# Tile starts at multiples of 256 bytes, and products that stream their columns backwards

## The chip, the cores and the metric

The kernel runs on one core of a Trainium2 chip. The metric is the device time of one execution in microseconds (us); lower is better. Five engines work beside each other, each with its own queue of instructions, and wait for one another through semaphores: TensorE (PE; its weight loads are listed as PEld), VectorE (DVE), ScalarE (ACT), GpSimd (POOL) and SyncE (SP), which issues the DMA transfers. SBUF is the on-chip memory of 128 partitions in which tiles lie; PSUM is the memory into which TensorE writes its products.

## The reference

Two layers of a hybrid block over a sequence of 512 positions and 1024 features, in float32. In each layer x gets, one after the other, the (normed) output of a mixer and of a feed-forward:

```python
for l in range(DEPTH):                       # DEPTH = 2
    mixed = hybrid_mixer(rms_norm(x, mix_pre_g[l]), w_in[l], ..., w_out[l])
    x = x + rms_norm(mixed, mix_post_g[l])
    ff = conv_ffn(rms_norm(x, ffn_pre_g[l]), w_up[l], conv_w[l], conv_b[l], w_down[l])
    x = x + rms_norm(ff, ffn_post_g[l])
```

`hybrid_mixer` projects to 3600 columns (`w_in`), runs dilated attention with 8 heads over one half and a bidirectional mLSTM with 4 heads over the other, and projects back with `w_out` (1024 x 1024). `conv_ffn` projects to 5632 columns (`w_up`), convolves three neighbouring positions, takes gelu(gate) * value and projects the 2816 columns back (`w_down`).

## The kernel before

Activations lie transposed: features on the 128 partitions, the 512 positions along the free dimension. The matrix x is 8 such tiles, `w_up` makes 44 of them, and so on. A weight tile of 128 x 1024 (8 blocks of 128 x 128) comes by DMA into a ring of three (`wraw`); ScalarE rounds it to a high part (`whi`, line 153) and VectorE subtracts that to get a low part (`wlo`, line 91), both float32r. Activations are split in the same way: `ah`/`al` (made in `parts_of`) for the two projections that read x, `cp` for the output projection, `hh`/`hl` for the 22 hidden tiles of the feed-forward. A product of full precision is then three matmuls, in `mac` (lines 200 to 202): weights high x moving high, weights low x moving high, weights high x moving low, all accumulating in one PSUM tile (`mm`, `o`, `s` or `t`, each one bank of 512 float32 columns). Each of the three loads its own 128 x 128 weights first.

`mac` runs with 512 columns in most places, and with `cols`, a half of 256 columns, in `first_group` (the first tiles after a norm) and `last_tiles` (the last tiles ahead of a norm), so that norm work of one half lies beside products of the other. The value projection (`proj_v`, lines 896 to 898) is the other way round: there the activations are the stationary operand and two weight blocks side by side (256 columns) are the moving one. The remaining matmuls are written out where they are used: gates (454, 456), attention scores (713, 714), transposes (730 and others), attention output (756), the mLSTM (787 to 839), the sums of squares (314) and the row of norm factors (329).

The order of the work is written by hand. `mac` calls `settle()`, which issues the norm steps that have come due by a count of streamed columns; two `Stream` objects feed pieces of attention and mLSTM work between the projections' matmuls in the mixer (`pump`). The feed-forward is a plain loop over tiles, in which VectorE and ScalarE do the convolution and the gelu of one pair of tiles under the products of the next.

Tiles come from pools. A pool takes its tiles in the order in which they are first asked for, each right behind the last, with starts at multiples of 32 bytes. The pools that matter here are `const`, `base` (x, `ah`, `al`), `wraw_p`, `whi_p`, `wlo_p`, `sm`, and one pool for each mixer (`mp`) and each feed-forward (`fp`, with `hh` and `hl`). The first tiles in `const` are two of 276 float32 per partition (`prm`, 1104 bytes), so most later tiles do not start at a multiple of 256 bytes.

Of the kernel before, what the change touches and what calls it, by code (L numbers as in the profile page):

```python
# [8 lines left out]
F32 = mybir.dt.float32  # L9
# [7 lines left out]
P = 128  # L17
# [6 lines left out]
FT = FF // P  # L24
EPS = 1e-6
RAW = 3
RING = 3
HD = 128
KSC = HD ** -0.5
# [25 lines left out]
NC1 = CC["rowmask"]  # L55


@with_exitstack
def tile_hybrid_block(ctx: ExitStack, tc: tile.TileContext, xt, w_in, w_g, w_out, w_up, w_down, par, cst, out):
    nc = tc.nc  # L60
    pool = lambda name, bufs=1, **kw: ctx.enter_context(tc.tile_pool(name=name, bufs=bufs, **kw))
    const = pool("const")
    base = pool("base")
    wraw_p = pool("wraw", RAW)
    whi_p = pool("whi", RING)
    wlo_p = pool("wlo", RING)
    sm = pool("sm", 2)
    pp = pool("pp", space=PSUM)

    def mm_ps():  # L70
        return pp.tile([P, T], F32, tag="mm", bufs=3, name="mm")
# [7 lines left out]
    def s_ps():  # L79
        return pp.tile([P, T], F32, tag="s", bufs=2, name="s")  # L80
# [4 lines left out]
    def o_ps():  # L85
        return pp.tile([P, T], F32, tag="o", bufs=1, name="o")
# [85 lines left out]
    def take():  # L172
        return ready.popleft() if ready else split_w()

    def prefetch(n):
        while len(ready) < n and raw_q:
            ready.append(split_w())
# [8 lines left out]
    def settle(all=False):  # L186
        due.sort(key=lambda e: e[0])
        while due and (all or due[0][0] <= clock[0]):
            with tc.issue_after(clock[1]):
                due.pop(0)[1]()  # L190

    def mac(ps, w, kk, rhs, first, last, cols=None):

        settle()
        clock[0] += 3 * (T if cols is None else cols.stop - cols.start)
        hi, lo = w[kk]
        rh, rl = rhs
        if cols is not None:
            rh, rl = rh[:, cols], rl[:, cols]
        nc.tensor.matmul(out=ps, lhsT=hi, rhs=rh, start=first, stop=False)  # L200
        nc.tensor.matmul(out=ps, lhsT=lo, rhs=rh, start=False, stop=False)  # L201
        clock[1] = nc.tensor.matmul(out=ps, lhsT=hi, rhs=rl, start=False, stop=last).ins  # L202


    class Stream:


        def __init__(self, rate):
            self.normal = rate
            self.gens = deque()  # L210
            self.due = 0.0
# [202 lines left out]
    def first_group(ws, pss, xp, scale, extra=None):  # L414

        for hf in range(2):
            cols = halves[hf]
            for k in range(KT):
                if hf == 1 and k == 0:
                    scale.go(0)  # L420
                if extra is not None:
                    extra(k, cols)
                for w, ps in zip(ws, pss):
                    mac(ps[:, cols], w, k, xp[k], k == 0, k == KT - 1, cols)
# [21 lines left out]
    def mixer_first(l, xp, sp, G, more, whole=False):  # L446
        gps = mm_ps()
        wg = wgs[l]
        ws = [take() for _ in range(G)]
        pss = [mm_ps() if m < 2 else o_ps() for m in range(G)]  # L450
        scale = PreScale(sp() if callable(sp) else sp)

        def gate_macs(k, cols):
            nc.tensor.matmul(out=gps[0:32, cols], lhsT=wg[:, k, 0:32], rhs=xp[k][0][:, cols], start=(k == 0), stop=False,
                             skip_group_check=True)
            nc.tensor.matmul(out=gps[0:16, cols], lhsT=wg[:, k, 0:16], rhs=xp[k][1][:, cols], start=False,
                             stop=(k == KT - 1), skip_group_check=True)

        if whole:

            for k in range(KT):
                if k == 5:
                    scale.go(0)
                    scale.go(1)
                gate_macs(k, slice(0, T))
                for w, ps in zip(ws, pss):
                    mac(ps, w, k, xp[k], k == 0, k == KT - 1)
        else:
            first_group(ws, pss, xp, scale, gate_macs)
        if more:  # L470
            scale.go(1)
            w = take()
            prefetch(RING - 1)
            ps = s_ps()
            for k in range(KT):
                mac(ps, w, k, xp[k], k == 0, k == KT - 1)
            pss.append(ps)
            settle(True)
        return gps, pss, scale, more or whole

    def mixer(l, xp, first, mp, post):
# [21 lines left out]
        def scale_ready():  # L503
            settle(True)
            if not more:
                scale.sums(1)
                scale.rows(1)
            nc.vector.tensor_tensor(out=cosr, in0=cosr, in1=scale.row, op=ALU.mult)
            nc.vector.tensor_tensor(out=sinr, in0=sinr, in1=scale.row, op=ALU.mult)
# [352 lines left out]

        prefetch(RING - 1)
        scale_ready()
# [5 lines left out]
        def proj():  # L870
            if pss:
                return pss.pop(0)
            w = take()
            prefetch(RING - 1)
            ps = mm_ps()
            for k in range(KT):
                mac(ps, w, k, xp[k], k == 0, k == KT - 1)
                M.pump()
                A.pump()
            return ps  # L880

        def proj_v():

            ws = [take()["all"] for _ in range(2)]
            prefetch(1)
            vps = []
            for c in range(4):
                if c % 2 == 0:
                    vps.append(mm_ps())
                o_ = vps[-1][:, (c % 2) * 2 * P:(c % 2 + 1) * 2 * P]  # L890
                for k in range(KT):
                    hi, lo = (w[:, 2 * (k % 4):2 * (k % 4) + 2, :].rearrange("p i f -> p (i f)") for w in ws[k // 4])
                    xh, xl = (t[:, c * P:(c + 1) * P] for t in xp[k])
                    settle()
                    clock[0] += 6 * P
                    nc.tensor.matmul(out=o_, lhsT=xh, rhs=hi, start=(k == 0), stop=False)  # L896
                    nc.tensor.matmul(out=o_, lhsT=xh, rhs=lo, start=False, stop=False)  # L897
                    clock[1] = nc.tensor.matmul(out=o_, lhsT=xl, rhs=hi, start=False, stop=(k == KT - 1)).ins  # L898
                    if k % 2:
                        M.pump()  # L900
                        A.pump()
            return vps

        M.start(gates(gps), .6)
        for r in range(4):
            done = set()
            for c in ORDER[r]:
                if c == "V":
                    vps = proj_v()
                    M.run()  # L910
                    A.run()
                    v_out(vps)
                elif c in "qk":
                    conv_out(proj(), r + 4 * (c == "k"), "m" + c)
                else:
                    ps = proj()
                    A.run()
                    rot_out(ps, "aq" if c == "a" else "ak")
                done.add(c)
                if done >= set("qkV") and "M" not in done:  # L920
                    M.run()
                    M.start(mlstm(r))
                    done.add("M")
                if done >= set("abV") and "A" not in done:
                    A.start(attn(r), AR[r])
                    done.add("A")
        for r in range(4):
            ps = proj()
# [49 lines left out]
        for m in range(G):  # L978
            mac(pss[m], ws[m], order[7], cp[order[7]], False, True)
        prefetch(RING)  # L980
        for m in range(G):
# [6 lines left out]
        for m in range(G, KT - 2):  # L988
            w = take()
            ps = o_ps() if m == G else mm_ps()  # L990
# [26 lines left out]
    def ffn_first(post):  # L1017
        ws = [take() for _ in range(FG)]
        pss = [mm4_ps() for _ in range(FG)]
        scale = PreScale(post.st2)  # L1020
        xp = post.ops
        first_group(ws, pss, xp, scale)
        return pss, scale
# [114 lines left out]
        gains(l)  # L1138
    first = None
    for l in range(DEPTH):  # L1140
        with tc.tile_pool(name=f"mix{l}", bufs=1) as mp:
            post = Post(l, "mix_post", l, "ffn_pre", 2)
            if first is None:
                first = mixer_first(l, xp, sp, 2, False, True)
            mixer(l, xp, first, mp, post)
            first = ffn_first(post)
            xp = post.ops
        with tc.tile_pool(name=f"ffn{l}", bufs=1) as fp:
            post = Post(l, "ffn_post", l + 1, "mix_pre", 1)
            ffn(l, xp, first, fp, post)  # L1150
            xp, sp = post.ops, lambda p=post: p.st2
            if l + 1 < DEPTH:
                first = mixer_first(l + 1, xp, sp, 2, False)
# [99 lines left out]
```

## Time and profile before

| | |
|---|---|
| time, median of 2 runs | 1366.78 us (1366.04 to 1367.51) |
| profiled execution, its own time | 1366.06 us |
| its span, first to last instruction | 1364.3 us |
| granted TensorE clock, mean | 0.998 |
| PE busy | 1329.2 us, 97% of the span, 7152 matmuls |
| PEld busy (weight loads, beside the matmuls) | 1127.2 us, 83% |
| VectorE busy | 955.4 us, 70% |
| ScalarE busy | 719.4 us, 53% |
| DMA | 115.34 MB, mean 85 GB/s |

The profile comes from one execution. In its timeline a row gives the start and the duration in us, the engine, the line of the kernel, the operation, the tile written and the tiles read, and the shape. Matmuls are pipelined and their ends are modelled, so the records of consecutive matmuls overlap; the distance between two starts says how long one occupies TensorE. The list of groups gives for each line and form the number of instructions, their busy time and the mean duration.

### The profile page before, as it was taken

What the parts mean: (1) busy time and instruction counts of PE and PEld (TensorE: products, weight loads), DVE (VectorE), ACT (ScalarE), POOL (GpSimd) and SP (SyncE); (2) the same over time, 40 slices, a digit from 0 to 9 for tenths busy, and PEclk for the clock granted to TensorE, in tenths of its full rate; (3) what the DMA queues carried; (4) which work ended last, traced back from release to release, by engine and by line L of the source; (5) the groups of instructions that cost most, each with busy time, mean ns of one, the idle gap of its engine ahead of it and who ended that gap; (6) DMA issues with size and microseconds to landing.
All of it is one profiled execution on the core that took longest, in us unless ns stands there. A gap on an engine that the chain in (4) does not pass through costs nothing. (4 is left out here: it accounts for less than half of the span.)

```text
span 1364.3 us, 18689 instructions
## 1 busy us (share of the span) xinstructions
PE 1329.2 (97%) x7152; PEld 1127.2 (83%) x7152; DVE 955.4 (70%) x1885; ACT 719.4 (53%) x1226; POOL 109.4 (8%) x116
## 2 busy tenths in 40 slices
PE   7999999999999999999989999999999999999997
PEld 6788879889888888888977888888898888888886
DVE  6999888847887777422499998887469777763233
ACT  5596696654644444323346867966446444442220
POOL 0000100024000000001130001000330000000002
PEclk9999999999999999999999999999999999999999
DMA  6212112241233333333222222122313333332321
GB/s 235 63 47 78 35 58 78 73 128 46 68 103 104 97 93 91 98 87 110 94 69 62 62 63 62 47 79 82 104 47 94 106 95 93 96 101 86 97 85 62
DMA packets 34089, 115.34 MB, mean 85 GB/s; under 512 B 3664, under 2 KB 6352, under 8 KB 34000
## 3 DMA queue, kind: packets, MB, share of 16 engines
q1 hardware_dynamic: 34000, 114.15, 27.6%
q8 instruction: 56, 0.92, 0.3%
q14 instruction: 33, 0.27, 0.1%
HBM read 112.04 MB, written 2.10 MB: 84 GB/s over the span
## 5 line engine op out<-in xcount | busy, mean ns | idle before, releaser
L91 DVE TENSOR_TENSOR wlo<-wraw,whi 128x1024 fp32r<-128x1024 f32 (+1 forms) x192 | 236.6, 1235 | 179.5 <-ACT whi L153 177.6
L200 PE MATMUL mm<-ah,whi 128*128 128x512 f32 (+1 forms) x880 | 336.4, 383 | 0.0
L201 PE MATMUL mm<-ah,wlo 128*128 128x512 f32 (+1 forms) x880 | 334.1, 380 | 0.0
L202 PE MATMUL mm<-al,whi 128*128 128x512 f32 (+1 forms) x880 | 332.9, 379 | 0.9 <-DVE al L348 0.8
L153 ACT CAST whi<-wraw 128x1024 fp32r<-128x1024 f32 (+1 forms) x192 | 197.6, 1034 | 166.7 <-PE mm L202 111.0
L202 PEld LDWEIGHTS mm<-al,whi 128*128 128x128 f32 x880 | 165.8, 189 | 30.5 <-DVE al L348 1.7
L200 PEld LDWEIGHTS mm<-ah,whi 128*128 128x128 f32 x880 | 166.2, 189 | 29.2 <-ACT whi L153 0.5
L201 PEld LDWEIGHTS mm<-ah,wlo 128*128 128x128 f32 x880 | 166.1, 189 | 27.5
L296 POOL TENSOR_TENSOR acc<-acc,sq 128x512 f32<-128x512 f32 x22 | 29.6, 1345 | 758.8 <-ACT sq L293 754.6
L201 PE MATMUL mm<-hh,wlo 128*128 128x512 f32 x220 | 86.8, 395 | 0.0
L202 PE MATMUL mm<-hl,whi 128*128 128x512 f32 x220 | 86.8, 395 | 0.0
L200 PE MATMUL mm<-hh,whi 128*128 128x512 f32 x220 | 86.8, 395 | 0.0
L1032 DVE TENSOR_TENSOR u<-mm,prow 128x512 f32<-128x512 f32 x64 | 43.8, 687 | 50.1 <-PE mm L202 39.6
L896 PE MATMUL mm<-whi,ah 128*128 128x256 f32 x256 | 73.6, 289 | 0.2 <-DVE cu L634 0.2
L1049 ACT CAST hh<-cv 128x512 fp32r<-128x512 f32 x44 | 27.3, 621 | 87.5 <-DVE cv L1046 87.5
L898 PE MATMUL mm<-whi,al 128*128 128x256 f32 x256 | 72.5, 284 | 0.0
L897 PE MATMUL mm<-wlo,ah 128*128 128x256 f32 x256 | 72.5, 283 | 0.0
L1044 ACT ACTIVATE cg<-cg 128x512 f32<-128x512 f32 x44 | 27.9, 633 | 74.5 <-DVE cg L1038 74.3
L201 PE MATMUL o<-ah,wlo 128*128 128x512 f32 (+1 forms) x160 | 60.7, 379 | 0.0
L202 PE MATMUL o<-al,whi 128*128 128x512 f32 (+1 forms) x160 | 60.6, 379 | 0.0
L200 PE MATMUL o<-ah,whi 128*128 128x512 f32 (+1 forms) x160 | 60.6, 379 | 0.0
L722 ACT ACTIVATE p<-p,mx 128x512 f32<-128x512 f32 x64 | 46.1, 720 | 18.0 <-DVE mx L719 17.9
(320 smaller groups left out, 2786.5 us busy)
## 6 DMA issues: line engine op xcount, KB each, us to landing
wraw<-in_w_up SPq DMA_DIRECT2D x88, 512.0 KB, 3.6
wraw<-in_w_in SPq DMA_DIRECT2D x56, 512.0 KB, 3.6
wraw<-in_w_down SPq DMA_DIRECT2D x32, 512.0 KB, 3.5
wraw<-in_w_out SPq DMA_DIRECT2D x16, 512.0 KB, 3.6
wraw<-in_w_down SPq DMA_DIRECT2D x16, 384.0 KB, 3.1
x<-in_xt SPq DMA_DIRECT2D x4, 512.0 KB, 7.0
out_dram<-x SPq DMA_DIRECT2D x8, 256.0 KB, 2.2
tb<-in_cst SPq DMA_DIRECT2D x2, 967.0 KB, 5.1
```

The lines of the kernel that those rows point to most:

```text
L91: nc.vector.tensor_tensor(out=dst, in0=src, in1=f32v(hi), op=ALU.subtract)
L153: nc.scalar.copy(out=hi[:, 0:m, :], in_=raw[:, k:k + m, :])
L200: nc.tensor.matmul(out=ps, lhsT=hi, rhs=rh, start=first, stop=False)
L201: nc.tensor.matmul(out=ps, lhsT=lo, rhs=rh, start=False, stop=False)
L202: clock[1] = nc.tensor.matmul(out=ps, lhsT=hi, rhs=rl, start=False, stop=last).ins
L296: e.tensor_tensor(out=self.acc[:, cols], in0=self.acc[:, cols], in1=sq, op=ALU.add)
L722: nc.scalar.activation(out=p_, in_=p_, func=AF.Exp, scale=-1.0, bias=mx, accum_out=den)
L896: nc.tensor.matmul(out=o_, lhsT=xh, rhs=hi, start=(k == 0), stop=False)
L897: nc.tensor.matmul(out=o_, lhsT=xh, rhs=lo, start=False, stop=False)
L898: clock[1] = nc.tensor.matmul(out=o_, lhsT=xl, rhs=hi, start=False, stop=(k == KT - 1)).ins
L1032: nc.vector.tensor_tensor(out=u, in0=ps, in1=st["row"], op=ALU.mult)
L1044: nc.scalar.activation(out=g, in_=g, func=AF.Gelu_apprx_tanh)
```

## The change

Three things change. A small class `Lines` stands between the code and the pools: it sends tiles of less than 256 bytes per partition to a pool of their own, rounds the size of the others up to a multiple of 256 bytes, and so makes each of them begin at a multiple of 256 (three filler tiles move the pools' beginnings to such a multiple). The matmuls of `mac` get their output, and both their moving operands, as reversed views (`[:, ::-1]`): the last column is read first and written first, and every column still goes to its own place. The matmuls of `proj_v` get the same. The stationary operands and all other matmuls stay as they are.

```diff
--- before.py
+++ after.py
@@ -24,6 +24,7 @@
 FT = FF // P
 EPS = 1e-6
 RAW = 3
+LINE = 256
 RING = 3
 HD = 128
 KSC = HD ** -0.5
@@ -55,16 +56,39 @@
 NC1 = CC["rowmask"]
 
 
+class Lines:
+
+
+    def __init__(self, pool, small, bufs=1):
+        self.pool, self.small, self.bufs = pool, small, bufs
+
+    def tile(self, shape, dtype, bufs=None, **kw):
+        bufs = bufs or self.bufs
+        n = 1
+        for s in shape[1:]:
+            n *= s
+        if n * 4 < LINE:
+            return self.small.tile(shape, dtype, bufs=bufs, **kw)
+        if n * 4 % LINE == 0:
+            return self.pool.tile(shape, dtype, bufs=bufs, **kw)
+        flat = self.pool.tile([shape[0], -(-n * 4 // LINE) * LINE // 4], dtype, bufs=bufs, **kw)[:, 0:n]
+        if len(shape) == 2:
+            return flat
+        names = "abcd"[:len(shape) - 1]
+        return flat.rearrange(f"p ({' '.join(names)}) -> p {' '.join(names)}", **dict(zip(names, shape[1:-1])))
+
+
 @with_exitstack
 def tile_hybrid_block(ctx: ExitStack, tc: tile.TileContext, xt, w_in, w_g, w_out, w_up, w_down, par, cst, out):
     nc = tc.nc
-    pool = lambda name, bufs=1, **kw: ctx.enter_context(tc.tile_pool(name=name, bufs=bufs, **kw))
-    const = pool("const")
-    base = pool("base")
-    wraw_p = pool("wraw", RAW)
-    whi_p = pool("whi", RING)
-    wlo_p = pool("wlo", RING)
-    sm = pool("sm", 2)
+    pool = lambda name, **kw: ctx.enter_context(tc.tile_pool(name=name, bufs=1, **kw))
+    big, small = pool("big"), pool("small")
+
+    big.tile([P, 32], F32, name="fill")
+    small.tile([P, 56], F32, name="fill_small")
+    const, sm = Lines(big, small), Lines(big, small, 2)
+    base = const
+    wraw_p, whi_p, wlo_p = Lines(big, small, RAW), Lines(big, small, RING), Lines(big, small, RING)
     pp = pool("pp", space=PSUM)
 
     def mm_ps():
@@ -197,6 +221,8 @@
         rh, rl = rhs
         if cols is not None:
             rh, rl = rh[:, cols], rl[:, cols]
+
+        ps, rh, rl = ps[:, ::-1], rh[:, ::-1], rl[:, ::-1]
         nc.tensor.matmul(out=ps, lhsT=hi, rhs=rh, start=first, stop=False)
         nc.tensor.matmul(out=ps, lhsT=lo, rhs=rh, start=False, stop=False)
         clock[1] = nc.tensor.matmul(out=ps, lhsT=hi, rhs=rl, start=False, stop=last).ins
@@ -887,12 +913,13 @@
             for c in range(4):
                 if c % 2 == 0:
                     vps.append(mm_ps())
-                o_ = vps[-1][:, (c % 2) * 2 * P:(c % 2 + 1) * 2 * P]
                 for k in range(KT):
+                    o_ = vps[-1][:, (c % 2) * 2 * P:(c % 2 + 1) * 2 * P]
                     hi, lo = (w[:, 2 * (k % 4):2 * (k % 4) + 2, :].rearrange("p i f -> p (i f)") for w in ws[k // 4])
                     xh, xl = (t[:, c * P:(c + 1) * P] for t in xp[k])
                     settle()
                     clock[0] += 6 * P
+                    o_, hi, lo = o_[:, ::-1], hi[:, ::-1], lo[:, ::-1]
                     nc.tensor.matmul(out=o_, lhsT=xh, rhs=hi, start=(k == 0), stop=False)
                     nc.tensor.matmul(out=o_, lhsT=xh, rhs=lo, start=False, stop=False)
                     clock[1] = nc.tensor.matmul(out=o_, lhsT=xl, rhs=hi, start=False, stop=(k == KT - 1)).ins
@@ -1138,14 +1165,18 @@
         gains(l)
     first = None
     for l in range(DEPTH):
-        with tc.tile_pool(name=f"mix{l}", bufs=1) as mp:
+        with tc.tile_pool(name=f"mix{l}", bufs=1) as mb, tc.tile_pool(name=f"mixs{l}", bufs=1) as ms:
+            mp = Lines(mb, ms)
             post = Post(l, "mix_post", l, "ffn_pre", 2)
             if first is None:
                 first = mixer_first(l, xp, sp, 2, False, True)
             mixer(l, xp, first, mp, post)
             first = ffn_first(post)
             xp = post.ops
-        with tc.tile_pool(name=f"ffn{l}", bufs=1) as fp:
+        with tc.tile_pool(name=f"ffn{l}", bufs=1) as fb:
+            fp = Lines(fb, fb)
+            if l == 1:
+                fb.tile([P, 16], F32, name="fill_ffn")
             post = Post(l, "ffn_post", l + 1, "mix_pre", 1)
             ffn(l, xp, first, fp, post)
             xp, sp = post.ops, lambda p=post: p.st2
```

## The prediction

> **What bounds the kernel now.** I read the top of the page first, then who TensorE waited for, then the matmuls in order of time.
>
> ```profile
> span 1364.3 us, 18689 instructions
> PE 1329.2 (97%) x7152; PEld 1127.2 (83%) x7152; DVE 955.4 (70%) x1885; ACT 719.4 (53%) x1226; POOL 109.4 (8%) x116
> PEclk9999999999999999999999999999999999999999
> ```
>
> TensorE is busy 97% of the span at a full granted clock; VectorE, next, 70%. The profiled execution took 1366.06 us, its span 1364.3 us, so 1.8 us lie around it; the median of the runs, 1366.78 us, is 0.7 us higher. I count from 1366.06.
>
> ```profile
> PE mm L454 <- ACT ah L347: 8.6, 3, 7.1
> PE s L329 <- DVE rs_y L266: 4.6, 4, 2.0
> PE t L562 <- DVE U L560: 3.3, 2, 1.7
> ```
>
> These are TensorE's largest waits (total us, times, longest): 7.1 us is the start, before the first activations exist, and the rest are norm and gate chains. Nothing there is worth 2%. What remains is the pace of the matmuls. The duration column doesn't give it, since records overlap; the distance between starts does. Here are first and last rows of four unbroken stretches.
>
> ```profile
> 460.14 0.39 PE L200 MATMUL mm<-ah,whi 128*128 128x512 f32 x1
> ...
> 465.35 0.39 PE L202 MATMUL mm<-al,whi 128*128 128x512 f32 x1
> 600.22 0.40 PE L200 MATMUL mm<-hh,whi 128*128 128x512 f32 x1
> ...
> 605.82 0.40 PE L200 MATMUL mm<-hh,whi 128*128 128x512 f32 x1
> 704.44 0.28 PE L896 MATMUL mm<-whi,ah 128*128 128x256 f32 x1
> ...
> 705.99 0.28 PE L897 MATMUL mm<-wlo,ah 128*128 128x256 f32 x1
> 661.33 0.28 PE L202 MATMUL mm<-hl,wlh 128*128 128x256 f32 x1
> ...
> 664.05 0.28 PE L202 MATMUL mm<-hl,wlh 128*128 128x256 f32 x1
> ```
>
> Up projection: 5.21 us over 23 steps, **226.5 ns** per 512-column product. Down projection: 5.60 us over 24 steps, **233.3 ns** for the same shape. Value projection: 1.55 us over 13 steps, **119.2 ns** per 256 columns. Last tile of the down projection: 2.72 us over 24 steps, **113.3 ns**. So one shape has two paces, 6.8 ns apart at 512 columns and 5.9 at 256, at one clock and with no wait. What differs between the first two stretches is where the tiles lie. Adding up the pools' tiles in the code, ah, al, whi and wlo start 160 bytes past a multiple of 256, while hh and hl start 96 past. And it is not the address alone:
>
> ```profile
> 668.62 0.28 PE L201 MATMUL o<-hh,wll 128*128 128x256 f32 x1
> ...
> 669.09 0.28 PE L202 MATMUL o<-hl,wlh 128*128 128x256 f32 x1
> 460.14 0.19 PEld L201 LDWEIGHTS mm<-ah,wlo 128*128 128x128 f32 x1
> ```
>
> The same form over the same kind of tiles now steps 0.47 us in 4, 117.5 ns, after other products had come between. The load of the next weights starts with the product (460.14, as in the matmul row above). Two streams that start together, each reading its own tile, whose joint pace depends on their addresses and can lock at two values: I read this as the weight load holding up the moving read a fixed number of times per product, each worth some 6.7 ns. That is my inference; no row names it.
>
> **The change part by part.** It removes and adds no instruction, DMA or semaphore; no step is moved past a queue and no wait is added. `Lines` only changes where tiles begin, and `[::-1]` only the direction in which `mac` and the value projection stream. The same columns reach the same places, and who reads the output waits for the end of the group as before.
>
> How many products are turned:
>
> ```profile
> 0.00:1364.00 1364.00, 622.00 (x1660) 312.89 (x1660) 1.00 0.28 85
> L200 PE MATMUL mm<-ah,whi 128*128 128x512 f32 x768 | 304.4, 396 | 0.0
> L200 PE MATMUL mm<-hh,whi 128*128 128x512 f32 x220 | 86.8, 395 | 0.0
> L200 PE MATMUL o<-ah,whi 128*128 128x512 f32 x144 | 56.1, 390 | 0.0
> L200 PE MATMUL o<-hh,whi 128*128 128x512 f32 x88 | 34.7, 394 | 0.0
> L200 PE MATMUL mm<-cp,whi 128*128 128x512 f32 x80 | 31.5, 398 | 0.0
> L896 PE MATMUL mm<-whi,ah 128*128 128x256 f32 x256 | 73.6, 289 | 0.2 <-DVE cu L634 0.2
> ```
>
> The first row is L200's alone over the whole span (busy of products and of weight loads, with counts): 1660. The five 512-column rows hold 768 + 220 + 144 + 88 + 80 = 1300; the other 360 I count as 256 columns wide (a few small groups are not, which moves the sum by under 0.5 us). L201 and L202 have as many, so 3900 wide products, 3 x (220 + 88) = 924 of them at 233.3 ns (hh, hl) and 2976 at 226.5, and 3 x 360 + 3 x 256 = 1848 narrow ones. Scores, transposes, gate products and the mLSTM's are not turned.
>
> *Alignment alone.* It gives moving tile and weights the same start modulo 256, as the up projection has today (160 and 160). Least: the 924 of hh and hl drop to 226.5 ns, 924 x 6.8 = 6.3 us. It could also cost: no row has both at 0, and the locking shows that pairs count; the other end is that the other 2976 take 233.3 ns, 2976 x 6.8 = 20 us lost.
>
> *Direction.* No product in the trace reads backwards. The nearest rows are a scan pair on VectorE, one forward, one with all operands reversed:
>
> ```profile
> L569 DVE TENSOR_TENSOR_SCAN cm<-ut x2: 412/413/414, 54.5 to 729.7; 32x128 f32<-32x128 f32 x2
> L570 DVE TENSOR_TENSOR_SCAN cb<-ut x2: 388/388/389, 54.9 to 730.1; 32x128 f32<-32x128 f32 x2
> ```
>
> Reversed is 388 ns against 413: a backward walk over fp32 in SBUF costs nothing by itself there. So I take direction to change only how the moving read meets the weight read. From above it is bounded by two steps: 226.5 - 2 x 6.7 = 213 ns; from below by two steps the other way, 240 ns. Which of them no row decides. I take **one step better than the best pace seen**, 220 ns wide, and for narrow ones the best pace seen, 113.3 ns, because it is the value nearest to the rows among those in which direction does anything good, and because with one start for all tiles every pair meets alike, so that one pace must hold for all. That its sign is a gain is a choice: the rows show that meetings cost, not which direction has fewer.
>
> Sum: 2976 x 6.5 = 19.3 us; 924 x 13.3 = 12.3; narrow, without the 264 of the last down tiles (which already touch 113.3), 1584 x 5.9 = 9.3; those 264 at half of 117.5 - 113.3, 0.6. Together 41.5 us.
>
> *What is late next.*
>
> ```profile
> 40.00:180.00 140.00, 134.90 (x804) 114.94 (x802) 126.69 (x310) 102.60 (x198) 9.49 (x6) 1.00 0.21 61
> 330.00:530.00 200.00, 200.00 (x905) 166.48 (x904) 151.32 (x208) 93.95 (x118) 0.00 (x0) 1.00 0.32 96
> 695.00:870.00 175.00, 167.78 (x1036) 144.27 (x1035) 157.25 (x394) 126.08 (x246) 13.51 (x14) 1.00 0.22 65
> ```
>
> Busy us by stage of PE, PEld, DVE, ACT, POOL. In the mixers (first and third row) VectorE is busy 126.69 of 140 us and 157.25 of 175, about 90%: faster products there run into its chains. About a thousand products are turned in these two stretches, so some 6 us of gain lie there; I let a third be lost, 2 us. In the feed-forward (second row) VectorE has a quarter of the time free, so the gain stays.
>
> Other engines: I expect no change of theirs from the new addresses.
>
> ```profile
> L153 ACT CAST whi<-wraw x192: 832/1051/1079, 8.1 to 1321.3; 128x1024 fp32r<-128x1024 f32 x178, 128x768 fp32r<-128x768 f32 x14
> L153 ACT CAST pth<-wraw x4: 1047/1048/1050, 268.1 to 948.4; 128x1024 fp32r<-128x1024 f32 x4
> wraw<-in_w_up SPq DMA_DIRECT2D x88, 512.0 KB, 3.6
> ```
>
> The same cast takes 1051 ns into whi (160 past) and 1048 into pth (192 past). Weight transfers land in 3.6 us, while a block of 24 products at 226.5 ns takes 5.4: hidden, and still hidden at 5.3. Without that cover a late block would stall TensorE for the difference. At the start the 7.1 us wait may move by some tenths.
>
> Result: 1366.06 - 41.5 + 2 = **1327 us**. Its own range: with 213 ns, 2976 x 13.2 + 924 x 20 + 9.9 - 2 = 65.7 us, 1300; and 1339, 2% below today, where it passes into the next case. (2%, 27 us, is about what a measurement of this kernel tells from no change.)
>
> **The rivals.**
>
> *A: direction does nothing*, alignment levels the paces: 924 x 6.8 = 6.3 us, perhaps 10 more if the narrow ones go to 113.3: 1350 to 1360. For it: the scan rows, and that up projections already have equal offsets and still need 226.5. [...] That the change doesn't do what it says (tiles of one pool off the grid) also ends here, near 1366.
>
> *B, slower: the backward read meets the weight read more often.* Two streams that move towards each other meet more often than two in one direction, if the load runs upwards. Place: every turned product. Two steps, 240 ns: 2976 x 13.5 + 924 x 6.7 + 1848 x 5.9 = 57 us, 1423; one step, 233.3: 20 + 11 = 31 us, 1397. It is slower by 2% once the mean cost passes 27 us / 5748 = 4.8 ns per turned product.
>
> *C, much slower: the output side doesn't take descending columns at full rate.* No row bounds it; at half rate 3900 x 226.5 ns = 883 us more, 2250 us. The scan rows speak against it, but they write SBUF, not an accumulating PSUM bank. [...]
>
> **How the numbers follow.** Forecast 50%; A 24% and the change without effect 2%; B 17%; C 7%. Faster by over 2%: 0.50; within 2%: 0.26; slower: 0.24. The range 1300 to 1400 takes in the forecast, A, and B with one step (8 of its 17), leaving out B's second step, C and some of the forecast's lower tail: about 80%.
>
> **What would show it.** Wide starts in both projections of the feed-forward at one distance: 220 ns right, 226.5 rival A, 233 or 240 B, over 400 C. The narrow ones at 113. VectorE's and ScalarE's durations unchanged, and their waits for TensorE shorter. The prediction is wrong if the up and down projection still differ (addresses aren't what sets the pace), or if the wide pace falls and the span doesn't, which would put the loss into TensorE's waits in the mixers.

## The result and the profile after

The changed kernel takes **1380.70 us** (median of 2 runs, 1379.93 to 1381.46) against 1366.78; the ratio is 1.0104 (95% interval 1.0087 to 1.0121). It is slower by 1%, well outside the noise, where 1327 us, 3% faster, had been forecast. The profiled execution took 1379.93 us, 13.9 us more than the one before.

The head of the page of the changed kernel and TensorE's largest wait (total us, times, longest us):

```profile
span 1377.9 us, 18691 instructions
PE 1344.9 (98%) x7152; PEld 1127.8 (82%) x7152; DVE 955.8 (69%) x1885; ACT 715.6 (52%) x1226; POOL 108.7 (8%) x116
PEclk9999999999999999999999999999999999999999
PE mm L480 <- ACT ah L373: 8.2, 3, 6.7
```

TensorE is busy 15.7 us longer with the same 7152 matmuls, at the same granted clock (0.998); its largest waits are what they were (the first 8.2 us against 8.6, the next two 4.6 and 3.3 as before), and no other engine's busy time moved by more than 4 us. So the loss is in the pace of the products. The timeline of the changed kernel, first and last rows of unbroken stretches (`mac` is at lines 226 to 228 now, the value projection at 923 to 925):

```profile
469.96 0.40 PE L226 MATMUL o<-ah,whi 128*128 128x512 f32 x1
...
475.56 0.40 PE L226 MATMUL mm<-ah,whi 128*128 128x512 f32 x1
609.96 0.40 PE L226 MATMUL mm<-hh,whi 128*128 128x512 f32 x1
...
615.56 0.40 PE L226 MATMUL mm<-hh,whi 128*128 128x512 f32 x1
711.04 0.28 PE L924 MATMUL mm<-wlo,ah 128*128 128x256 f32 x1
...
712.46 0.28 PE L924 MATMUL mm<-wlo,ah 128*128 128x256 f32 x1
```

Up projection 5.60 us over 24 steps, **233.3 ns** (226.5 before). Down projection 5.60 us over 24 steps, 233.3 ns (233.3 before). Value projection 1.42 us over 12 steps, 118.3 ns (119.2 before). In these stretches all wide products run at one pace, as the prediction said they must, but it is the worse of the two that were there. Summing the distances between starts over the whole trace, the turned wide products took 15.9 us more, the turned narrow ones 0.2 us less, and the pauses over 0.4 us 1.6 us less.

### The profile page after: what moved, and what is told of

Its sections match the earlier page's. It is cut to its first block, busy times and chain, and to the rows that moved or that the text cites. A ratio compares the mean times of both kernels' runs of the same rounds, so it can differ in the third digit from the quotient of the medians.

```text
span 1377.9 us, 18691 instructions
## 1 busy us (share of the span) xinstructions
PE 1344.9 (98%) x7152; PEld 1127.8 (82%) x7152; DVE 955.8 (69%) x1885; ACT 715.6 (52%) x1226; POOL 108.7 (8%) x116
## 5 line engine op out<-in xcount | busy, mean ns | idle before, releaser
L226 PE MATMUL mm<-ah,whi 128*128 128x512 f32 (+1 forms) x880 | 341.1, 388 | 0.0
L227 PE MATMUL mm<-ah,wlo 128*128 128x512 f32 (+1 forms) x880 | 339.1, 386 | 0.0
L228 PE MATMUL mm<-al,whi 128*128 128x512 f32 (+1 forms) x880 | 337.7, 385 | 0.8 <-DVE al L374 0.8
```

## The experiments

The theories after the result: (1) the backward read is what costs; (2) the common start on the 256-byte grid is what costs; (3) the two reads, of weights and of moving tile, meet in a way that depends on both starts and the direction.

**Grid without direction (e1).**

```diff
-        ps, rh, rl = ps[:, ::-1], rh[:, ::-1], rl[:, ::-1]
...
-                    o_, hi, lo = o_[:, ::-1], hi[:, ::-1], lo[:, ::-1]
```

> The changed kernel with both reversed reads taken back: tiles on the 256-byte grid, products forward. Theory one (the backward read is what costs): wide products at 226.5 ns in both projections of the feed-forward, time 1366 - 924 x 6.8 ns = about 1360 us. Theory two (the common start of moving tile and weights on the grid is what costs, the direction does nothing): 233.3 ns everywhere as in the changed kernel, about 1381 us. Theory three (pace depends on both starts and the direction together): a third value is possible, 213 to 240 ns.

Measured: 1360.99 us, ratio 0.9963 (0.9950 to 0.9977). Its timeline, the down projection of the first layer and that of the second:

```profile
609.93 0.39 PE L227 MATMUL mm<-hl,whi 128*128 128x512 f32 x1
...
615.37 0.39 PE L227 MATMUL o<-hl,whi 128*128 128x512 f32 x1
1290.01 0.39 PE L227 MATMUL mm<-hl,whi 128*128 128x512 f32 x1
...
1295.50 0.39 PE L227 MATMUL mm<-hl,whi 128*128 128x512 f32 x1
```

5.44 us over 24 steps, 226.7 ns, and the up projection steps as fast; in the second layer 5.49 us, 228.8 ns. There the filler of 64 bytes in the changed kernel pushes the hidden tiles 64 past the grid, so this part of the change doesn't do what it says. Theory two falls: on the grid and forward, products run at the better pace.

**Direction without grid (e2).** The same two lines added to the kernel before.

> The kernel before with only the reversed reads and writes added, tiles where they were (starts 160 past a multiple of 256 for activations of x and weights, 96 past for the hidden tiles). Theory one (a backward read costs a step of 6.7 ns wherever the tile lies): up projection 233.3 ns, down projection 240 ns, 1366 + 2976 x 6.8 + 924 x 6.7 ns = about 1392 us. Theory two (only the grid costs): 226.5 and 233.3 ns as before, 1366 us. Theory three (starts and direction together): the two projections change by different amounts or signs.

Measured: 1379.86 us, ratio 1.0102 (1.0088 to 1.0116).

```profile
469.93 0.40 PE L202 MATMUL o<-ah,whi 128*128 128x512 f32 x1
...
475.53 0.40 PE L202 MATMUL mm<-ah,whi 128*128 128x512 f32 x1
609.93 0.40 PE L202 MATMUL mm<-hh,whi 128*128 128x512 f32 x1
...
615.53 0.40 PE L202 MATMUL mm<-hh,whi 128*128 128x512 f32 x1
```

233.3 ns in both, at starts of 160 and of 96. Not theory one as I had put it (a step on top, 240 ns in the down projection): going backwards is one pace of its own, which takes what good placement had given and adds nothing where placement was bad. That is a case of theory three: the up projection changes by 6.7 ns, the down projection by none. With e1 this accounts for the change: the grid gives 4.9 us (1365.91 to 1360.99), the direction takes 19.7 (1360.99 to 1380.70, from two sets of runs). With the products going backwards the common start was worth nothing: e2 without it took 1379.86 us, the changed kernel with it 1380.70.

**A map of paces (m1).** Products alone, 18 in a row for each setting (the run holds 186 settings, 8 more than its expectation says):

> No block at all: 18 products in a row on one loaded tile for each of 178 settings, and x is copied to the output. Swept are the start of the moving tile and of the weights modulo 256 (a is 0, b is 32, up to h, 224; first letter moving, second weights), forward (f) and reversed (r), 512 columns (wide) and 256 (half), weight loads of 32, 64 and 96 columns instead of 128 (loadq, loadh, loadt), only the moving read or only the output reversed (mvonly, outonly), and starts off by 4 to 24 bytes (fine). Theory A (weight load and moving read meet): the wide pace depends on the pair of starts, and falls with a shorter weight load towards 213 ns; fff is 226.5, fdf 233.3, raa 233.3. Theory B (the moving read alone pays for where it starts and which way it goes): the pace depends on the first letter and the direction alone, the same for every second letter and every length of weight load. Theory C (the output side pays for the direction): outonly is slower than forward, mvonly is not.

The matmuls of one setting are merged in a row; from its start to the next row's are 18 products. Forward with the moving tile at d (96), weights at d, e, f, then two of the same reversed:

```profile
126.17 4.28 PE L43 MATMUL fwide_dd<-mv,wt 128*128 128x512 f32 x18
130.29 4.35 PE L43 MATMUL fwide_de<-mv,wt 128*128 128x512 f32 x18
134.48 4.36 PE L43 MATMUL fwide_df<-mv,wt 128*128 128x512 f32 x18
...
398.42 4.36 PE L43 MATMUL rwide_de<-mv,wt 128*128 128x512 f32 x18
402.62 4.36 PE L43 MATMUL rwide_df<-mv,wt 128*128 128x512 f32 x18
```

Forward, equal starts take 4.12 us for 18, unequal ones 4.19 (the row of de); reversed it is 4.20. Means of the last 12 distances between starts within each setting, in ns, moving tile at 96:

| weights at | 0 | 32 | 64 | 96 | 128 | 160 | 192 | 224 |
|---|---|---|---|---|---|---|---|---|
| forward | 233.3 | 228.8 | 233.3 | 227.5 | 233.3 | 233.3 | 233.8 | 231.7 |
| reversed | 233.3 | 233.3 | 233.3 | 233.3 | 233.3 | 233.3 | 233.3 | 233.3 |

At equal starts the first products are slower, and the last ones stand at 226.7. The other rows of the map repeat this, shifted (but for aa, the first setting of the run, whose first products stand 427 ns apart): forward, the distance of the two starts modulo 256 decides (good are equal starts, 227.5 ns in this row, and the moving tile 64 further, 228.8); reversed, all 64 pairs give 233.3. The starts are not all, though: with the moving tile 64 further, m2 below gave 233.3 forward (mfwf_ca) where this map gave 228.9 for the same pair, so something besides the starts counts as well; what ran before is one candidate, and no run tests it.

Read backwards, a tile begins at its last column, 2044 bytes behind its start, so in none of the 64 reversed pairs did the first address read equal the weights' start modulo 256. One setting with the moving tile 4 bytes past did have it equal (rfine_four) and took 235.6 ns; the same tile forward took 236.7, 3.4 above the 233.3 of most unequal starts, so a start 4 bytes off costs by itself. This speaks against an unlucky first address as the cause of the backward pace, but doesn't rule it out. The two halves of the backward step taken apart, and the weight load shortened:

```profile
549.64 4.37 PE L43 MATMUL mvonly_aa<-mv,wt 128*128 128x512 f32 x18
553.84 4.37 PE L43 MATMUL mvonly_ff<-mv,wt 128*128 128x512 f32 x18
...
562.25 4.26 PE L43 MATMUL outonly_aa<-mv,wt 128*128 128x512 f32 x18
566.35 3.83 PE L43 MATMUL outonly_ff<-mv,wt 128*128 128x512 f32 x16
...
624.49 4.36 PE L43 MATMUL rloadq_aa<-mv,wt 128*32 128x512 f32 x18
628.68 4.37 PE L43 MATMUL rloadh_aa<-mv,wt 128*64 128x512 f32 x18
```

Only the moving read backwards: 4.20 us, 233.3 ns. Only the output backwards: 4.10 us, and 226.7 ns over its last 12, the pace of forward products at equal starts: writing downwards cost nothing. A quarter of the weight columns to load: still 4.19 us. So theory C of the run falls; of the other two, B holds backwards and falls forward, and A falls backwards. Shorter loads going forward didn't come down to 213 ns either; at equal starts (aa) they gave 230.0 to 231.7, more than the full load, and at 96 against 160 (df) 228.5 to 232.2, less than its 233.3.

**Walking and standing reads (m2).**

> No block: 18 products in a row for each setting, x is copied to the output. mf and mr: moving read forward or reversed; wf: weights as usual, wo: weights are one column repeated 128 times, so that their read doesn't walk; letters as before (start of moving, start of weights). cols a to h: 512 down to 288 columns in steps of 32. block: blocks of 2 to 256 columns in descending order, ascending inside. bcast: moving is one column repeated; two: every second column; same: one moving tile again and again. Theory A (two walking reads that meet): with wo the reversed pace leaves 233.3 and the forward pace stops depending on the starts; bcast comes near 213 ns. Theory B (the backward moving read has a cost of its own): mrwo stays at 233.3, and the cost of cols r over cols f is either the same at every width (a cost per product, 6.7 ns) or in proportion to the width (a cost per column). Blocks: with B and a cost per turn of direction, small blocks cost more; if only the last address counts, every block size costs the same as reversed.

```profile
25.35 4.36 PE L51 MATMUL mrwo_aa<-mv,wt 128*128 128x512 f32 x18
29.55 4.25 PE L51 MATMUL mfwf_ff<-mv,wt 128*128 128x512 f32 x18
33.64 4.32 PE L51 MATMUL mfwo_ff<-mv,wt 128*128 128x512 f32 x18
37.80 4.37 PE L51 MATMUL mrwf_ff<-mv,wt 128*128 128x512 f32 x18
```

With weights that stand still (wo) the backward pace stays at 4.20 us for 18, 233.3 ns (mrwo_aa; the same at all six pairs of starts). Forward at equal starts it goes from 4.09 to 4.16, and no longer depends on the starts (231.1 to 231.7 at all six). So walking weights do change the forward pace, as I had inferred, but also for the better: equal starts (226.7) beat weights that don't walk at all (231.1 to 231.7), while most unequal ones (233.3) are worse. Backwards it is 233.3 with walking and with standing weights. Against a forward read beside standing weights that is about 2 ns more (233.3 against 231.1 to 231.7); the rest of the 6.7 ns is the gain of equal starts (231.1 to 226.7), which the backward read doesn't get.

```profile
182.54 4.37 PE L51 MATMUL block_sixteen<-mv,wt 128*128 128x512 f32 x18
186.75 4.27 PE L51 MATMUL block_sixtyfour<-mv,wt 128*128 128x512 f32 x18
190.85 4.24 PE L51 MATMUL block_quarter<-mv,wt 128*128 128x512 f32 x18
...
199.01 4.05 PE L51 MATMUL bcast_a<-mv,wt 128*128 128x512 f32 x18
202.90 8.32 PE L51 MATMUL two_f<-mv,wt 128*128 128x512 f32 x18
211.04 8.58 PE L51 MATMUL two_r<-mv,wt 128*128 128x512 f32 x18
219.44 4.28 PE L51 MATMUL last_f<-mv,wt 128*128 128x512 f32 x18
```

Descending blocks of 16 columns: 4.21 us, the pace of single columns backwards. Blocks of 64, ascending inside: 4.10, as good as forward. One moving column repeated: 3.89 us, 215.8 ns. I take that as an estimate of TensorE's pace when the moving read doesn't hold it up; by that the forward read at equal starts (226.7) adds 11 ns to it and the backward one (233.3) 17.5. At 256 columns a repeated column took 111.7 ns (bcast_half, m3), 3.8 more than half of 215.8. Every second column, over 4 KB instead of 2: 8.14 us forward and 8.40 backwards, twice each pace. In m3, 256 columns taken every second one, over the 2 KB of a wide product, took 230.0 ns forward and 233.3 backwards, about as long as 512 dense ones. So in these settings the pace followed the bytes that the moving read spans, 2 or 4 KB, and not the number of columns it takes. That a wide product lasts as long as this read was my inference; no run measures the read by itself.

Widths, of which 320 and 288 columns are shown:

```profile
134.36 2.80 PE L51 MATMUL colsf_g<-mv,wt 128*128 128x320 f32 x18
137.00 2.54 PE L51 MATMUL colsf_h<-mv,wt 128*128 128x288 f32 x18
...
160.81 2.81 PE L51 MATMUL colsr_g<-mv,wt 128*128 128x320 f32 x18
163.46 1.76 PE L51 MATMUL colsr_h<-mv,wt 128*128 128x288 f32 x12
```

At 320 columns 18 products take 2.64 us forward and 2.65 reversed. By the last 12 distances the cost is neither one per product nor one per column: 6.7 ns at 512 (settled), 2.6 to 3.9 from 480 down to 384, 1.0 at 352, nothing at 320, 1.6 at 288. The narrow products of the kernel have 256, and m1 has settings for them:

```profile
708.66 2.32 PE L43 MATMUL fhalf_aa<-mv,wt 128*128 128x256 f32 x18
710.81 2.29 PE L43 MATMUL fhalf_ba<-mv,wt 128*128 128x256 f32 x18
...
727.87 2.23 PE L43 MATMUL fhalf_df<-mv,wt 128*128 128x256 f32 x18
729.94 2.29 PE L43 MATMUL rhalf_aa<-mv,wt 128*128 128x256 f32 x18
```

Forward, equal starts are the slow ones at this width: 2.15 us for 18, 120.0 ns, at aa, against 2.07 us, 113.3 ns, at 96 and 160 (df). Reversed, the ten settings gave 117.8 to 120.0 ns. So the common start, which helps wide products (233.3 to 226.7 ns), takes away the best place of narrow ones (113.3 to 120.0).

**Equal starts off the grid (e4).** The kernel before with one line at the head of each feed-forward pool:

```diff
+            fp.tile([P, 16], F32, name="shift")
```

> The kernel before, with one filler tile of 64 bytes at the head of each feed-forward pool and nothing else: the hidden tiles then start 160 past a multiple of 256, as the weights do, and nothing lies on the grid. Equal starts are what counts: down projection 226.5 ns instead of 233.3, 924 x 6.8 = 6.3 us, about 1360 us. The 256-byte grid is what counts: 233.3 ns as before, 1366 us.

Measured: 1361.11 us, ratio 0.9961 (0.9947 to 0.9975); down projection:

```profile
609.93 0.39 PE L201 MATMUL mm<-hh,wlo 128*128 128x512 f32 x1
...
615.37 0.39 PE L201 MATMUL o<-hh,wlo 128*128 128x512 f32 x1
```

5.44 us over 24 steps, 226.7 ns, with both starts at 160. Equal starts are what counts, not the grid; 64 bytes do what the class `Lines` does (1361.11 us here, 1360.99 in e1).

**All of it on the grid, forward (e3).** e1 without the filler of 64 bytes in the second layer.

> Forward products on the grid as in e1, and also the second layer's feed-forward tiles, which the changed kernel's filler puts 64 bytes past it, moved onto the grid. If the distance of the two starts sets the forward pace, the second layer's hidden products go from about 229 to 226.5 ns: 462 wide products x 2.4 ns = 1.1 us under e1, about 1360 us, ratio to before 0.995. If the grid itself doesn't matter, the same as e1.

Measured: 1360.29 us, ratio 0.9956 (0.9943 to 0.9968). In the second layer:

```profile
1289.92 0.39 PE L227 MATMUL mm<-hl,whi 128*128 128x512 f32 x1
...
1295.36 0.39 PE L227 MATMUL mm<-hl,whi 128*128 128x512 f32 x1
```

226.7 ns instead of 228.8. Its time and e1's can't be told apart (their runs overlap), but the pace moved as expected. This version beats both kernels: by 0.44% the one before.

**Backwards in blocks (e5).** The changed kernel with its reversed views replaced by views in descending blocks of 64 columns:

```diff
-        ps, rh, rl = ps[:, ::-1], rh[:, ::-1], rl[:, ::-1]
+        ps, rh, rl = (t.rearrange("p (b c) -> p b c", c=64)[:, ::-1, :] for t in (ps, rh, rl))
...
-                    o_, hi, lo = o_[:, ::-1], hi[:, ::-1], lo[:, ::-1]
+                    o_, hi, lo = (t.rearrange("p (b c) -> p b c", c=64)[:, ::-1, :] for t in (o_, hi, lo))
```

> The changed kernel, still from the last column to the first, but in blocks of 64 columns (256 bytes) that are read and written upwards inside. If what costs is the backward walk from one column to the next inside 64 columns, wide products come back to about 226.5 ns and the time to that of e1, 1361 us (ratio to before 0.996). If the order of the whole tile costs (last part first), 233.3 ns stay and 1380 us (1.010).

Measured: 1361.02 us, ratio 0.9957 (0.9944 to 0.9971):

```profile
469.98 0.39 PE L227 MATMUL o<-ah,wlo 128*128 128x512 f32 x1
...
475.42 0.39 PE L227 MATMUL mm<-ah,wlo 128*128 128x512 f32 x1
```

226.7 ns, and the whole 19.7 us are back. So it cost nothing that the last part comes first; the loss is gone once the walk goes upwards inside 64 columns. (Blocks of 64 differ from single columns in a second way too: their first address is again equal to the weights' start modulo 256. The next run bears on it.)

**Block sizes (m3).**

> No block, x is copied to the output; 512-column products whose moving read and output go through blocks of 8, 16, 32, 64 or 128 columns in descending order, ascending inside, at equal starts of 0, 64, 128 and 160 bytes past a multiple of 256 and at 128 against 0. If the step belongs to leaving a stretch of some fixed size downwards, there is one block size from which the pace is 226.7 ns, below it 233.3; if that stretch is tied to addresses, the size at which it turns depends on the start.

The last letters are the starts of moving tile and weights, e is 128:

```profile
25.54 4.34 PE L51 MATMUL bthirty_aa<-mv,wt 128*128 128x512 f32 x18
29.71 4.29 PE L51 MATMUL bsixty_aa<-mv,wt 128*128 128x512 f32 x18
33.84 4.24 PE L51 MATMUL bquarter_aa<-mv,wt 128*128 128x512 f32 x18
...
108.70 4.26 PE L51 MATMUL bthirty_ea<-mv,wt 128*128 128x512 f32 x18
112.80 4.35 PE L51 MATMUL bsixty_ea<-mv,wt 128*128 128x512 f32 x18
116.99 4.36 PE L51 MATMUL bquarter_ea<-mv,wt 128*128 128x512 f32 x18
```

At equal starts of 0, 64, 128 and 160 alike: blocks of 8 and 16 columns 233.3 ns, of 32 232.5, of 64 226.7 over the last seven distances, of 128 226.7. At 128 against 0, blocks of 32 gave 226.7 and blocks of 64 and 128 gave 233.3: the first address read there, in blocks of 32, is again a multiple of 256 as the weights' is. In these settings the good pace went with where the read begins, not with where the tile does. So there is no one size at which it turns: at equal starts, blocks of 8, 16 and 32 begin 32, 64 and 128 bytes away from a match, those of 64 and 128 at one. Blocks of 32 are good (226.7) when they begin at a match; whether smaller ones would be was not run.

## Why the prediction was wrong

- **What bounds the kernel: right.** TensorE's pace, two paces (226.5 and 233.3 ns) at one clock (0.998), set by the tiles' places. The time of every kernel above moved with its wide pace: 1360.3 to 1361.1 us with 226.7 ns in the first layer's feed-forward (e1, e3, e4, e5), 1379.9 and 1380.7 with 233.3 (e2, the changed kernel). That there would be one pace came out by luck: it was to follow from the common start, but the second layer's hidden tiles don't have that start, and e2 has the one pace without it.
- **Alignment alone: right for wide products going forward.** 6.3 us were computed for levelling the hidden products; e1 gave 4.9, e4 4.8, e3 5.6. By the distances between starts, the wide products took 6.6, 6.1 and 6.8 us less than before and the narrow ones 1.2, 1.0 and 1.5 more. e1 also keeps 462 products of the second layer at 228.8 (about 1 us).
- **Direction: the step that failed.** I took "one step better than the best pace seen" because it was near the rows, and said that its sign was a choice. It had no row behind it. The sum took 220 ns for every wide product and got 19.3 and 12.3 us from it; the runs showed 233.3, a loss for the first group and no change for the second. The model under it (a fixed number of meetings with the weight load, which another direction might avoid) was wrong where it was used: m1 and m2 show that the backward pace doesn't know of the weights at all, neither of their start nor of the length of their load nor whether they walk (233.3 in each). Rows of VectorE couldn't show that a backward read misses the gain of equal starts (231.1 to 226.7 ns) and costs about 2 ns more than a forward one beside standing weights.
- **The narrow term failed too.** 9.9 us were to come from 113.3 ns everywhere; 0.2 us came. 113.3 had been read from forward products of the hidden tiles (96) with weights in tiles that `ah` and `al` had held (160). m1 gives it for just this pair going forward, and neither for equal starts nor backwards; in e4 and e3, forward at equal starts, the same products of the kernel mostly stand at 120.
- **The range held by luck.** 1380.70 lies in 1300 to 1400 because rival B's one step was let in at its upper end, not by the forecast's reasons.
- **The scan rows misled.** A backward walk cost VectorE nothing (388 against 413 ns), and I carried that to TensorE's moving read. There it cost 6.7 ns at equal starts (226.7 to 233.3, mvonly in m1).
- **Rival B had the outcome, not the reason.** Its price for one step, 233.3 ns on all wide products, is the measured pace; 2976 x 6.8 = 20.2 us against 15.9 summed from the trace, since not all of the 2976 had stood at 226.5 before: 2486 products of x between other wide ones of `mac` went from 227.4 to 233.5 ns in the mean, 15.2 us, but 280 of the output projection only from 231.8 to 233.8, and those with other work beside them hardly moved (0.1 us together). Its other 11 us, for the narrow products, didn't come: 0.2 us less instead. That makes 1380 and not 1397. Its mechanism, more meetings with the weight load, falls with the model: standing weights leave 233.3.
- **Rival A** gives e1's time, 1361, not the changed kernel's. That direction does nothing held for the down projection (233.3 ns before and after) and not for the up projection (226.5 to 233.3).
- **Rival C** falls: outonly, with descending columns on the output side alone, runs at 226.7 ns (m1).
- **What is late next** was not put to the test, since products got no faster. That the other engines and the transfers would not change was right: their busy times stand within 4 us and the transfers of `w_up` land in 3.5 us instead of 3.6.

Open: why forward reads are best at equal starts, and by what the reads of 512 columns lose 6.7 ns backwards but those of 320 none. Nor is there a run in which the weights are read backwards as well, or one in which the first address of a backward read matches without a start 4 bytes off. No run here takes that apart.

## What to carry to other kernels

Read the pace of a dense stretch from the distance between starts, by tile: two paces of one shape at one clock (here 226.5 and 233.3 ns) came from placement, and a filler of a few bytes that gives moving tile and weights the same start modulo 256 was worth 0.4% here, though the 256-column products lost about 1 us by it. Let the moving operand ascend, at least inside blocks of 64 columns (226.7 ns against 233.3); the order of such blocks (e5) and the direction of the output (m1) were free here. When a step of the sum has no row behind it, measure it alone first: a map of 64 placements in two directions fits into one run.

## What was not expected of the hardware

The pace of a float32r product of 512 columns changed with what its moving read covers and how: 215.8 ns with one column repeated, 226.7 forward at equal starts, 233.3 backwards, 452 (8.14 us for 18) when only every second column is read. And products whose weights walk can be faster than those whose weights stand: at equal starts 226.7 ns against 231.1, while at most other starts 233.3.
